# A diffusion block on one core: one of the seven block products of the MLP's second matrix product is itself made by seven inner products

## The chip, the cores and the metric

The kernel runs on one core of one Trainium2 chip. Its engines each work through a queue of their own: TensorE (PE in the profile, with its weight loads shown apart as PEld), VectorE (DVE), ScalarE (ACT), GpSimd (POOL) and SyncE (SP), which only issues transfers. The metric is the device time of one execution in microseconds. "Before" is the kernel without the change, 1021.87 us in the median of 3 runs (1021.27 to 1022.33).

## The reference, cut to what matters

One layer of a hybrid diffusion backbone. A token-mixing sub-layer (a pooling mixer and neighbourhood attention) comes first and is not touched; the second sub-layer is an MLP with a squared ReLU, on 1024 tokens of width 1024 with 4096 hidden columns, all in float32:

```python
def _sq_relu_mlp(h, w1, w2):
    return jnp.square(jax.nn.relu(h @ w1)) @ w2
...
    y_x = _sq_relu_mlp(_modulate(x, g_pre_mlp[l], sh2, sc2), w_mlp_in[l], w_mlp_out[l])
    x = x + gt2 * _rmsnorm(y_x, g_post_mlp[l])
```

The change concerns the second product alone: the hidden values (1024 x 4096) times `w_mlp_out` (4096 x 1024).

## The kernel before, in words

**Precision.** A float32 product is made of three matmuls in the fp32r type. Each operand is split into a high part (a cast, on ACT, `high_part`, L169) and a low part (operand minus high part, on DVE, `low_part`, L175), and `three` (L221 to L223) adds high x high, high x low and low x high in one PSUM bank.

**Seven block products.** The second product is cut in 2 x 2 blocks (512 tokens, 2048 hidden columns, 512 output columns) and made by Winograd's form of Strassen's method: the seven products P1 to P7 instead of eight. Their left operands are blocks of hidden values or sums of them (A11, A12, A22, S1 to S4), written to DRAM by the first product's stage (`keep`, on ACT's queue) and read back (`hidden`, tiles `hr...`, on SP's queue). Their right operands are blocks of `w_mlp_out` (`b11`, `b12`, `b21`, `b22`) or differences of them, made by DVE (L2047, L2049).

**Groups.** Each block product is 8 groups (g = 0 to 7) of 256 hidden columns. A group is 4 token tiles x 2 pieces x 3 matmuls, 24 matmuls of 128x512. P1 adds up in the four banks `pyx`, P6 in `pyy`; P2 is the block product A12 x b21, added in P1's banks, its groups between those of P6 (`items`). Then come P7, P5, P4 and P3 in the banks `pyv` and `pyz`.

**Order.** In this last stage PE, ACT, DVE and SP are held to the order in which the program is written (`in_order`); POOL's order is the scheduler's. Every group begins with `prepare()`, which writes down the loads, splits and sums for the group three items further on in the list `items`. So operands are made at most about three items ahead: the buffers of high and low weight parts (`whl`, 8 of 128x1024, four pairs) come free only when PE is through with the item four back. Raw weights have 4 buffers (`wraw`), raw hidden values 4 (`h`), and 33 pages (`act`) hold the rest. Loads are issued on SP's queue in the order of the program, so a load that waits for its buffer, or for an earlier transfer whose semaphore it is to use, holds up those behind it.

**The gate.** Among P1's groups the MLP's gate row is finished: before group 3 PE sums `accb` in the bank `pgb`, DVE multiplies it (L270), and POOL issues four small stores of it (`mod_out`, L276). Otherwise POOL has nothing to do in this stretch.

Of the kernel before, what the change touches and what calls it, by code (L numbers as in the profile page):

```python
# [11 lines left out]
F32 = mybir.dt.float32  # L12
# [91 lines left out]
def hybrid_block(ctx, tc, x, ctx_in, w_mod, mod_pages, w_u, b_mod, gp1, gp2, w_in, pool_w, rpb, w_out, w1, w2, vectors,  # L104
# [1414 lines left out]
    with tc.tile_pool(name="ps2", bufs=6, space=PSUM) as ps2:  # L1519

      def bank(name):
          if name[:3] == "phv" or name in ("poz_0", "poz_1") or name[:2] in ("px", "py") and name[-2:] in ("_3", "_7"):
              return lasting(name)
          return ps2.tile([P, 512], F32, tag="mm", name=name)

      with ExitStack() as tmp2:
# [257 lines left out]
        def second_steps(b12, b22):  # L1784
# [13 lines left out]
            for name in ("T2", "T1", "T3", "B22", "T4"):  # L1798
# [9 lines left out]
                for n in ("A11", "A12", "A22", "S1", "S2", "S3", "S4")}  # L1808
# [49 lines left out]
        def kept(name, p):  # L1858
            return hidd[name][p // 2][:, (p % 2) * 512 : (p % 2) * 512 + 512]
# [160 lines left out]
        def wcols(name, i, h, g):  # L2020
            return columns(wraw.tile([P, 1024], F32, tag="raw", name=f"{name}_{g}"), i, h, g)
# [15 lines left out]
        def operands(name, g, made=None):  # L2037
# [4 lines left out]
            if name == "P2":  # L2042
                return hidden("A12", g), made(f"b21_{g}", wcols("b21", 1, 0, g))
# [18 lines left out]

        AHEAD = 3
        items = [("P1", g) for g in range(NG)]
        for a, b in (("P6", "P2"), ("P7", "P5")):
            items += [(n, g) for g in range(NG) for n in (a, b)]
# [48 lines left out]
        with tc.issue_after(first[ET.PE]), in_order(ET.PE, ET.Activation, ET.DVE, ET.SP):  # L2115
# [67 lines left out]
            x = four("pyx")  # L2183
            for g in range(NG):
                if g == 1:
                    gain = mod_gain(gp2, page("gpb")[:, :256], nc.gpsimd)
                if g == 3:
                    mod_gate("b", acc_b[-1], gain, lambda name: pg)
                    mod_out("b", acc_b[-1])
                group(x, "P1", g)  # L2190
            s1 = halves("s1")
            for t in range(4):
                nc.scalar.copy(s1[t], x[t])
            y = four("pyy")
            for g in range(NG):
                group(y, "P6", g)
                if g == NG // 2:
                    G2 = gate_page("b")
                if g == NG - 1:
                    u2 = halves("u2")  # L2200
                    for t in range(4):
                        nc.vector.tensor_tensor(u2[t], y[t], s1[t], add)
                group(x, "P2", g, more=True)
            for t in range(4):
                rows[t] = page(f"row{t}")
                gated(t, 0, x[t])
# [93 lines left out]
```

## Time and profile before

| | us |
|---|---|
| median of 3 runs (lowest, highest) | 1021.87 (1021.27, 1022.33) |
| span of the profiled execution, first to last instruction | 1019.4 |
| what lies around the span (median less span) | 2.5 |
| PE busy in the span | 1008.7 |
| from P1's first matmul to P7's first | 131.3 |

The profiled execution's own time is known by its span alone, so a forecast is made against the span and 2.5 us are put on it. In the rows, buffer numbers are left out of names: `b_3l` is the low part of `b11` of group 3, `hhA_3h` the high part of its hidden block, and A11, A12 and A22 all read `hdA`, `hrA` or `hhA`. In a list of instructions the first number is the start and the second the duration, in us; a duration runs to the instruction's end, while the next one of a full queue starts a little earlier, so costs in a row of instructions are taken from start to start. `PEclk` is the granted share of TensorE's clock.

### The profile page before, as it was taken

What the parts mean: (1) busy time and instruction counts of PE and PEld (TensorE: products, weight loads), DVE (VectorE), ACT (ScalarE), POOL (GpSimd) and SP (SyncE); (2) the same over time, 40 slices, a digit from 0 to 9 for tenths busy, and PEclk for the clock granted to TensorE, in tenths of its full rate; (3) what the DMA queues carried; (4) which work ended last, traced back from release to release, by engine and by line L of the source; (5) the groups of instructions that cost most, each with busy time, mean ns of one, the idle gap of its engine ahead of it and who ended that gap; (6) DMA issues with size and microseconds to landing.
All of it is one profiled execution on the core that took longest, in us unless ns stands there. A gap on an engine that the chain in (4) does not pass through costs nothing.

```text
span 1019.4 us, 16277 instructions
## 1 busy us (share of the span) xinstructions
PE 1008.7 (99%) x6010; PEld 834.4 (82%) x6010; DVE 746.4 (73%) x1170; ACT 548.1 (54%) x964; POOL 154.5 (15%) x234
## 2 busy tenths in 40 slices
PE   8999999999999999999999999999999999999997
PEld 5788888878998888888888888888888888888886
DVE  5588767977885689879988888745757666557576
ACT  6672254348986746786555544555543343334442
POOL 4111210166774221410000000000000000000002
PEclk9999999999999999999999999999999999999999
DMA  9899798641448945885776657537967766556555
GB/s 368 314 295 305 256 265 293 206 104 43 96 95 204 232 183 187 297 216 197 256 260 208 213 194 225 177 135 251 347 218 261 248 228 214 200 167 203 169 184 226
DMA packets 117312, 222.72 MB, mean 218 GB/s; under 512 B 9521, under 2 KB 47281, under 8 KB 117233
## 3 DMA queue, kind: packets, MB, share of 16 engines
q1 hardware_dynamic: 90736, 171.14, 50.0%
q0 software_dynamic: 9360, 19.58, 9.3%
q10 hardware_dynamic: 17136, 30.97, 8.1%
q8 instruction: 47, 0.77, 0.3%
q14 instruction: 33, 0.26, 0.1%
HBM read 168.16 MB, written 52.45 MB: 216 GB/s over the span
## 4 chain that ended last, share of the span: by engine, by line
PE 96%; DMA 2%; DVE 1%; ACT 0%; issue 0%; SPq 0%; DVEq 0%; ACTq 0%
PE pu L476 4%; PE pa L1288 4%; PE S L1208 3%; PE phx L221 3%; PE phz L221 3%; PE phv L221 3%; PE pyx L221 3%; PE phx L223 3%; PE phx L222 3%; PE phv L223 3%; PE pyx L222 3%; PE pyz L221 3%; PE phz L223 3%; PE phv L222 3%; PE phz L222 3%; PE pyz L222 3%
## 5 line engine op out<-in xcount | busy, mean ns | idle before, releaser
L1234 ACT ACTIVATE sp<-sp,nm 128x640 f32<-128x640 f32 (+1 forms) x64 | 51.4, 802 | 10.9 <-DVE ri L1238 5.1
L1223 DVE CUSTOM_DVE_ANT_0 sp<-S,tab 128x640 f32<-128x640 f32 (+1 forms) x56 | 44.5, 795 | 13.9 <-PE pz L1254 9.5
L1855 ACT ACTIVATE c<-c 128x512 f32<-128x512 f32 x48 | 30.3, 632 | 44.8 <-DVE c L1975 25.6
L169 ACT CAST wpS<-S 128x512 fp32r<-128x512 f32 x64 | 38.7, 616 | 27.4 <-PE phv L223 9.7
L221 PE MATMUL phx<-thB,wpA 128*128 128x512 f32 x128 | 50.2, 392 | 0.0
L222 PE MATMUL phx<-tlB,wpA 128*128 128x512 f32 x128 | 49.8, 389 | 0.0
L223 PE MATMUL phx<-thB,wpA 128*128 128x512 f32 x128 | 49.8, 389 | 0.0
L175 DVE TENSOR_TENSOR wpS<-S,wpS 128x512 fp32r<-128x512 f32 x64 | 43.5, 688 | 7.6 <-ACT wpS L169 7.5
L163 POOL TENSOR_TENSOR ry<-vy,nhalf 128x1 f32<-128x1 f32 x7 | 5.4, 767 | 275.6 <-DVE vy L161 275.6
L1856 ACT ACTIVATE c<-c 128x512 f32<-128x512 f32 x48 | 30.3, 631 | 15.1 <-DVE sa L1938 12.1
L221 PEld LDWEIGHTS phx<-thB,wpA 128*128 128x128 f32 x128 | 24.0, 188 | 5.5 <-ACT s L1906 0.4
L223 PEld LDWEIGHTS phx<-thB,wpA 128*128 128x128 f32 x128 | 24.0, 188 | 5.0
L222 PEld LDWEIGHTS phx<-tlB,wpA 128*128 128x128 f32 x128 | 24.0, 188 | 4.9
L1273 DVE COPY pt<-T 128x512 f32<-128x512 f32 x32 | 22.0, 687 | 5.5 <-PE T L1254 5.5
L1288 PE MATMUL pa<-pt,v 128*64 128x128 f32 x352 | 25.9, 279 | 0.2
L221 PE MATMUL phv<-thT,wpA 128*128 128x512 f32 x64 | 25.0, 391 | 0.0
L221 PE MATMUL phz<-thB,wpS 128*128 128x512 f32 x64 | 25.0, 391 | 0.0
L223 PE MATMUL phv<-thT,wpA 128*128 128x512 f32 x64 | 24.9, 389 | 0.0
L222 PE MATMUL phz<-tlB,wpS 128*128 128x512 f32 x64 | 24.9, 389 | 0.0
L222 PE MATMUL phv<-tlT,wpA 128*128 128x512 f32 x64 | 24.9, 389 | 0.0
L221 PE MATMUL phy<-thT,wpS 128*128 128x512 f32 x64 | 24.9, 389 | 0.0
L222 PE MATMUL phy<-tlT,wpS 128*128 128x512 f32 x64 | 24.9, 389 | 0.0
(1179 smaller groups left out, 3442.6 us busy)
## 6 DMA issues: line engine op xcount, KB each, us to landing
b<-in_w SPq DMA_DIRECT2D x64, 512.0 KB, 4.3
hrS<-hdS SPq DMA_DIRECT2D x32, 512.0 KB, 5.1
hrA<-hdA SPq DMA_DIRECT2D x24, 512.0 KB, 5.6
wm<-in_mod_pages SPq DMA_DIRECT2D x16, 512.0 KB, 9.3
wa_0w<-in_w SPq DMA_DIRECT2D x16, 512.0 KB, 5.0
wa_1w<-in_w SPq DMA_DIRECT2D x16, 512.0 KB, 4.3
hdA<-c ACTq DMA_DIRECT2D x32, 256.0 KB, 2.2
hdS<-sa ACTq DMA_DIRECT2D x32, 256.0 KB, 2.2
```

The costliest lines, as they stand in the source:

```text
L169: nc.scalar.copy(hi, src)
L175: nc.vector.tensor_tensor(lo, src, hi.bitcast(F32), sub)
L221: nc.tensor.matmul(ps, ahi, bhi, start=first, stop=False, skip_group_check=more)
L222: nc.tensor.matmul(ps, ahi, blo, start=False, stop=False, skip_group_check=more)
L223: nc.tensor.matmul(ps, alo, bhi, start=False, stop=last, skip_group_check=more)
L476: nc.tensor.matmul(pus[b][j], wk(wgt, k, low, j * P, P), r, start=(k == 0 and n == 0), stop=(k == KT - 1 and n == 2))
L1208: nc.tensor.matmul(S[e][:, c0 : c0 + k[0].shape[1]], q[n_q][hs, cols], k[n_k][hs], start=(n_q + n_k == 0), stop=(n_q == 1))
L1223: nc.vector.tensor_tensor_reduce(out=to, in0=s, in1=bt, scale=1.0, scalar=BIG, op0=add, op1=ALU.min, accum_out=nm)
L1234: nc.scalar.activation(sp, sp, AF.Exp, bias=least[i, e], scale=-1.0, accum_out=sums[i][:, e : e + 1])
L1288: nc.tensor.matmul(pa[e * HD : (e + 1) * HD, cols], v[:, f : f + HD], turns[i][:, e, c] if c < 4 else fifths[i][:, :, (e + 1) * HD : (e + ...
L1855: nc.scalar.activation(r, src, AF.Relu)
L1856: nc.scalar.activation(r, r, AF.Square)
```

## The change

P2 is itself cut in 2 x 2 (256 tokens, 1024 hidden columns, 256 output columns) and made by seven inner products M1 to M7, in the same form. Each is made in two halves (h = 0, 1) of 512 hidden columns: 2 token tiles x 4 pieces x 3 matmuls, 24 matmuls of 128x256, all of one inner product in a single bank `pyi...`. The 14 halves stand no longer between P6's groups but among P1's and P6's: after P1's group 2 the order is M1 M1, P1, M5, P1, M5 M6, P1, M6, P1, M4 M4, P1 (the last group), M2 M2, P6, M3, P6, M3 M7, P6, M7, P6, and then P6's groups 4 to 7.

Left and right operands of an inner product are quarters of A12 and b21, or sums of such. Every half loads quarters of 512 KB (14 loads per h, 28 in all, where P2 had 16), the sums are made by POOL on 128x1024 (`inner_operands`: two for M5, two for M6, one for M4, one for M3, two for M7, for each h), and each half is split as before, on ACT and DVE. A12 is stored in two tensors `hidq` of DRAM instead of eight. Results are taken from the banks by ACT and DVE into pages (`inner_kept`), one sum of 128x512 among them by POOL, and the four row blocks that P1 and P2 together gave are added up by POOL (128x512, four) and not in PSUM. P1's and P6's last bank no longer stand in the two lasting banks, which the inner products use.

**POOL's queue around the gate's four loads (L266).** `accb` is the gate's sum and `gb` its stores; `Si`, `Ti` and `S1i` are pages that are kept, and the number behind them is h. Before:

```order
L238 MEMSET accb_7168 128x1024
L239 DMA accb_7168<-in_b_mod 1x16x64
L266 DMA gpb_8128<-in_gp2 32x256 x4
L276 DMA gb_8210<-accb_7168 16x1x16 x4
L163 TENSOR_TENSOR ry_0_10109<-vy_0_10107,nhalf_79 128x1
```

With the change:

```order
L266 DMA gpb_8122<-in_gp2 32x256 x4
L2086 TENSOR_TENSOR S1i_0_8199<-S1i_0_8199,a11M5_0_8201 128x1024
L2068 TENSOR_TENSOR Si_0_8086<-S1i_0_8199,Si_0_8086 128x1024
L2068 TENSOR_TENSOR Ti_0_8088<-b01M5_0_8203,Ti_0_8088 128x1024
L276 DMA gb_8283<-accb_7162 16x1x16 x4
L2086 TENSOR_TENSOR S1i_1_8288<-S1i_1_8288,a11M5_1_8290 128x1024
L2068 TENSOR_TENSOR Si_1_8127<-S1i_1_8288,Si_1_8127 128x1024
L2068 TENSOR_TENSOR Ti_1_8129<-b01M5_1_8292,Ti_1_8129 128x1024
L2068 TENSOR_TENSOR Ti_0_8088<-b11M6_0_8328,Ti_0_8088 128x1024
```

M6's left operand (`Si`) is made between M5's left (`S1i`) and right (`Ti`), and the gate's stores stand between the two halves of M5.

**DVE's queue at the same place.** `hhM5_0l` and `wM5_0l` are the low parts of M5's left and right operand for h = 0. With the change:

```order
L175 TENSOR_TENSOR hhM5_0l_8208<-S1i_0_8199,hhM5_0h_8207 128x1024
L175 TENSOR_TENSOR wM5_0l_8212<-Ti_0_8088,wM5_0h_8211 128x1024
L175 TENSOR_TENSOR hhA11_4l_8245<-hrA11_4_8242,hhA11_4h_8244 128x1024
L175 TENSOR_TENSOR b11_4l_8249<-b11_4_8240,b11_4h_8248 128x1024
L270 TENSOR_TENSOR accb_7162<-pgb_8081,gpb_8122 128x256
L175 TENSOR_TENSOR hhM5_1l_8297<-S1i_1_8288,hhM5_1h_8296 128x1024
L175 TENSOR_TENSOR wM5_1l_8301<-Ti_1_8129,wM5_1h_8300 128x1024
L175 TENSOR_TENSOR hhM6_0l_8333<-Si_0_8086,hhM6_0h_8332 128x1024
```

The gate's product, which POOL's stores wait for, is now behind both low parts of M5's first half and of P1's group 4.

## The diff

```diff
@@ -1519,7 +1519,8 @@
     with tc.tile_pool(name="ps2", bufs=6, space=PSUM) as ps2:
 
       def bank(name):
-          if name[:3] == "phv" or name in ("poz_0", "poz_1") or name[:2] in ("px", "py") and name[-2:] in ("_3", "_7"):
+          if (name[:3] in ("phv", "pyi") or name in ("poz_0", "poz_1") or name[:2] == "px" and name[-2:] in ("_3", "_7")
+                  or name in ("pyv_3", "pyz_3")):
               return lasting(name)
           return ps2.tile([P, 512], F32, tag="mm", name=name)
 
@@ -1805,7 +1806,8 @@
         EARLY, SPILLED = 10, 6
 
         hidd = {n: [dram.tile([P, 1024], F32, tag=f"hd{n}_{g}", name=f"hd{n}_{g}") for g in range(NPAIR // 2)]
-                for n in ("A11", "A12", "A22", "S1", "S2", "S3", "S4")}
+                for n in ("A11", "A22", "S1", "S2", "S3", "S4")}
+        hidq = [dram.tile([P, 4, 1024], F32, tag=f"hq{h}", name=f"hq{h}") for h in range(2)]
 
         s1d = [dram.tile([P, 512], F32, tag=f"s1_{p}", name=f"s1_{p}") for p in range(SPILLED)]
 
@@ -1856,6 +1858,8 @@
             nc.scalar.activation(r, r, AF.Square)
 
         def kept(name, p):
+            if name == "A12":
+                return hidq[p // 8][:, p // 2 % 4, (p % 2) * 512 : (p % 2) * 512 + 512]
             return hidd[name][p // 2][:, (p % 2) * 512 : (p % 2) * 512 + 512]
 
 
@@ -2039,8 +2043,8 @@
             if name == "P1":
                 t1[g] = columns(page(f"b11_{g}"), 0, 0, g)
                 return hidden("A11", g, g <= AHEAD + 1), made(f"b11_{g}", t1[g])
-            if name == "P2":
-                return hidden("A12", g), made(f"b21_{g}", wcols("b21", 1, 0, g))
+            if name in INNER:
+                return inner_operands(name, g)
             if name == "P6":
 
                 b12, b22 = wcols("b12", 0, 1, g), wcols("b22", 1, 1, g)
@@ -2060,10 +2064,53 @@
             nc.vector.tensor_tensor(b21, b21, t2[g], sub)
             return hidden("A22", g), made(f"t4_{g}", b21)
 
+        INNER = ("M1", "M5", "M6", "M4", "M2", "M3", "M7")
+        kept_raw, subtract = {}, lambda to, a, b: nc.gpsimd.tensor_tensor(to, a, b, sub)
+
+        def inner_raw(name, left, r, c, h, at=None):
+            if at is None:
+                at = tmp.tile([P, 1024], F32, tag="h", name=name, bufs=4) if left else wraw.tile([P, 1024], F32, tag="raw", name=name)
+            nc.sync.dma_start(at.rearrange("p (a f) -> p a f", a=4),
+                              hidq[h][:, :, c * 512 + r * 256 : c * 512 + r * 256 + 256] if left else
+                              w2v[1][:, 8 * h + r : 8 * h + 8 : 2, c * 256 : (c + 1) * 256])
+            return at
+
+        def inner_operands(name, h):
+            a = lambda r, c, at=None: inner_raw(f"a{r}{c}{name}_{h}", True, r, c, h, at)
+            b = lambda r, c, at=None: inner_raw(f"b{r}{c}{name}_{h}", False, r, c, h, at)
+            new = lambda n: kept_raw.setdefault((n, h), page(f"{n}i_{h}"))
+            if name == "M1":
+                x, y = a(0, 0, new("S")), b(0, 0, new("T"))
+            elif name == "M5":
+                x, more, y, less = a(1, 0, new("S1")), a(1, 1), kept_raw["T", h], b(0, 1)
+                nc.gpsimd.tensor_tensor(x, x, more, add)
+                subtract(y, less, y)
+            elif name == "M6":
+                x, y, z = kept_raw["S", h], kept_raw["T", h], b(1, 1)
+                subtract(x, kept_raw.pop(("S1", h)), x)
+                subtract(y, z, y)
+            elif name == "M4":
+                x, z, y = a(1, 1), b(1, 0, new("B21")), kept_raw.pop(("T", h))
+                subtract(y, z, y)
+            elif name == "M2":
+                x, y = a(0, 1, new("A12")), kept_raw.pop(("B21", h))
+            elif name == "M3":
+                x, z, y = kept_raw.pop(("S", h)), kept_raw.pop(("A12", h)), b(1, 1)
+                subtract(x, z, x)
+            else:
+                x, z, y, less = a(0, 0), a(1, 0), b(1, 1), b(0, 1)
+                subtract(x, x, z)
+                subtract(y, y, less)
+            return split_pages(f"hh{name}_{h}", x), high_low(f"w{name}_{h}", y)
+
         AHEAD = 3
-        items = [("P1", g) for g in range(NG)]
-        for a, b in (("P6", "P2"), ("P7", "P5")):
-            items += [(n, g) for g in range(NG) for n in (a, b)]
+        inner = iter([(n, h) for n in INNER for h in range(2)])
+        items = [("P1", g) for g in range(3)]
+        for n, i in zip((2, 1, 2, 1, 2, 2, 1, 2, 1), [("P1", g) for g in range(3, NG)] + [("P6", g) for g in range(4)]):
+            items += [*islice(inner, n), i]
+        items += [("P6", g) for g in range(4, NG)]
+        assert next(inner, None) is None
+        items += [(n, g) for g in range(NG) for n in ("P7", "P5")]
         items += [(n, g) for g in range(NG // 2) for n in ("P4", "P3")] + [("P3", g) for g in range(NG // 2, NG)]
         items += [("P4", g) for g in range(NG // 2, NG)]
         made = {}
@@ -2180,30 +2227,78 @@
 
 
             pg = bank("pgb")
-            x = four("pyx")
-            for g in range(NG):
-                if g == 1:
-                    gain = mod_gain(gp2, page("gpb")[:, :256], nc.gpsimd)
-                if g == 3:
-                    mod_gate("b", acc_b[-1], gain, lambda name: pg)
-                    mod_out("b", acc_b[-1])
-                group(x, "P1", g)
-            s1 = halves("s1")
+            inner_banks, parts = {}, {}
+            by_two = lambda v: v.rearrange("p (t n) -> p t n", t=2)
+
+            def inner_part(name):
+                if name not in parts:
+                    parts[name] = page(f"{name}i")
+                return parts[name]
+
+            block = lambda r, c: by_two(inner_part(f"c{r}"))[:, :, c * 256 : (c + 1) * 256]
+            held = lambda n: inner_part("tu"[n // 2])[:, n % 2 * 512 : n % 2 * 512 + 512]
+
+            def inner_kept(name, ps):
+                plus = lambda to, a, b: nc.vector.tensor_tensor(to, a, b, add)
+                if name == "M1":
+                    nc.scalar.copy(held(0), ps)
+                elif name == "M5":
+                    nc.scalar.copy(held(1), ps)
+                elif name == "M6":
+                    plus(held(2), ps, held(0))
+                    nc.gpsimd.tensor_tensor(held(3), held(2), held(1), add)
+                elif name == "M4":
+                    plus(block(1, 0), by_two(ps), by_two(held(2)))
+                elif name == "M2":
+                    plus(block(0, 0), by_two(ps), by_two(held(0)))
+                elif name == "M3":
+                    plus(block(0, 1), by_two(ps), by_two(held(3)))
+                else:
+                    plus(block(1, 0), by_two(ps), block(1, 0))
+                    plus(block(1, 1), by_two(ps), by_two(held(3)))
+
+            def inner_group(name, h):
+                prepare()
+                a, w = made.pop((name, h))
+                if h == 0:
+                    inner_banks[name] = bank(f"pyi{name}")
+                ps = inner_banks[name]
+                for t in range(2):
+                    for j in range(4):
+                        ts, cs = slice(j * 256 + t * P, j * 256 + (t + 1) * P), slice(j * 256, (j + 1) * 256)
+                        three(ps[:, t * 256 : (t + 1) * 256], a[0][:, ts], a[1][:, ts], w[0][:, cs], w[1][:, cs],
+                              h + t + j == 0, h == 1 and j == 3, more=t > 0)
+                if h == 1:
+                    inner_kept(name, ps)
+
+            x, y = four("pyx"), None
+            for name, g in items[: items.index(("P7", 0))]:
+                if name in INNER:
+                    inner_group(name, g)
+                elif name == "P1":
+                    if g == 1:
+                        gain = mod_gain(gp2, page("gpb")[:, :256], nc.gpsimd)
+                    if g == 3:
+                        mod_gate("b", acc_b[-1], gain, lambda name: pg)
+                        mod_out("b", acc_b[-1])
+                    group(x, "P1", g)
+                    if g == NG - 1:
+                        s1 = halves("s1")
+                        for t in range(4):
+                            nc.scalar.copy(s1[t], x[t])
+                        y = four("pyy")
+                else:
+                    group(y, "P6", g)
+                    if g == NG // 2:
+                        G2 = gate_page("b")
+            u2 = halves("u2")
             for t in range(4):
-                nc.scalar.copy(s1[t], x[t])
-            y = four("pyy")
-            for g in range(NG):
-                group(y, "P6", g)
-                if g == NG // 2:
-                    G2 = gate_page("b")
-                if g == NG - 1:
-                    u2 = halves("u2")
-                    for t in range(4):
-                        nc.vector.tensor_tensor(u2[t], y[t], s1[t], add)
-                group(x, "P2", g, more=True)
+                nc.vector.tensor_tensor(u2[t], y[t], s1[t], add)
             for t in range(4):
+                c = inner_part(f"c{t // 2}")[:, t % 2 * 512 : t % 2 * 512 + 512]
+                nc.gpsimd.tensor_tensor(c, c, s1[t], add)
                 rows[t] = page(f"row{t}")
-                gated(t, 0, x[t])
+                gated(t, 0, c)
             v, z = four("pyv"), four("pyz")
             for g in range(NG):
                 group(v, "P7", g)
```

## The prediction

> **What bounds the kernel now.** I read the page's busy shares first, then the stage's windows, then its instructions.
>
> ```profile
> span 1019.4 us, 16277 instructions
> PE 1008.7 (99%) x6010; PEld 834.4 (82%) x6010; DVE 746.4 (73%) x1170; ACT 548.1 (54%) x964; POOL 154.5 (15%) x234
> 707.80:752.10 44.30, 44.30 (x201) 36.11 (x200) 31.11 (x30) 22.43 (x25) 1.93 (x4) 1.00 0.83 295
> 752.10:839.10 87.00, 87.00 (x385) 72.06 (x384) 57.87 (x52) 34.38 (x39) 0.00 (x0) 1.00 0.71 240
> L221 PE MATMUL pyx<-b_0h,hhA_0h x16: 389/389/389, 707.8 to 762.3; 128*128 128x512 f32 x16
> L221 PE MATMUL pyv<-t_0h,hhS_0h x8: 389/389/389, 839.1 to 843.9; 128*128 128x512 f32 x8
> ```
>
> The two windows are P1's eight groups and then P6's and P2's sixteen (length, then busy time of PE, PEld, DVE, ACT, POOL, the granted clock, DMA's busy share, GB/s). PE is busy in all of both, so this stretch lasts as long as its matmuls; DVE is free for a third of it, POOL nearly all of it. The two tile rows give the stretch's ends: 839.1 - 707.8 = 131.3 us.
>
> **The matmuls.** The tail of the kernel already has this shape, 128x256 with a new weight load for each:
>
> ```profile
> 762.99 0.39 PE L221 MATMUL pyy<-t_1h,hhS_1h 128*128 128x512 f32 x1
> 768.43 0.39 PE L221 MATMUL pyx<-b_1h,hhA_1h 128*128 128x512 f32 x1
> 1010.66 0.28 PE L221 MATMUL pyw<-t_4h,hhA_4h 128*128 128x256 f32 x1
> 1013.42 0.28 PE L223 MATMUL pyw<-t_7h,hhA_7l 128*128 128x256 f32 x1
> ```
>
> The first two rows are 24 matmuls apart: 5.44 us a group, 0.2267 us for 512 columns. The last two are the first and last of 24: 2.76 / 23 = 0.1200 us for 256. P2 goes, 8 x 5.44 = 43.5 us; 14 halves of 24 x 0.12 = 2.88 us come, 40.3 us. **The gain on PE is 3.2 us**, all there is to gain. P1's eight groups took 44.3 us, 0.8 more than 8 x 5.44; that is the gate's sum.
>
> **What the halves need.** Splits and POOL's sums are costed by these rows:
>
> ```profile
> 716.45 1.22 DVE L175 TENSOR_TENSOR hhA_3l<-hrA,hhA_3h 128x1024 fp32r<-128x1024 f32 x1
> 717.58 1.22 DVE L175 TENSOR_TENSOR b_3l<-b,b_3h 128x1024 fp32r<-128x1024 f32 x1
> 756.15 1.22 DVE L2047 TENSOR_TENSOR b<-b,b 128x1024 f32<-128x1024 f32 x1
> 758.55 1.22 DVE L175 TENSOR_TENSOR hhS_2l<-hrS,hhS_2h 128x1024 fp32r<-128x1024 f32 x1
> 715.00 1.04 ACT L169 CAST hhA_3h<-hrA 128x1024 fp32r<-128x1024 f32 x1
> 715.95 1.05 ACT L169 CAST b_3h<-b 128x1024 fp32r<-128x1024 f32 x1
> 222.98 1.28 POOL L1091 TENSOR_TENSOR qP<-q,qP 128x512 fp32r<-128x512 f32 x1
> 224.22 0.28 POOL L1240 COPY rb<-ri 128x128 f32<-128x128 f32 x1
> 261.20 2.50 POOL L1077 TENSOR_TENSOR tab<-msk,U 128x128 f32<-128x128 f32 x6
> L276 POOL DMA_DIRECT2D gb<-accb x4 | 1.9, 490 | 27.3 <-DVE accb L270 27.3
> 725.99 0.42 DVE L270 TENSOR_TENSOR accb<-pgb,gpb 128x256 f32<-128x256 f32 x1
> ```
>
> From start to start: a low part 1.14 us, P6's two differences with the gap 2.40, a cast 0.95, the gate's four stores 1.96 of POOL's queue. POOL has no 128x1024 sum in this trace. Its 128x512 takes 1.25, its 128x128 2.50 / 6 = 0.42; the line through both gives 2.37 us. Twice the 512 row is 2.5; the slope without the fixed part, 2.23. I take 2.37.
>
> **The term that decides: DVE and POOL exclude each other.** Where both worked on operands in SBUF, the timeline reads:
>
> ```profile
> 211.89 0.68 DVE L175 TENSOR_TENSOR qP<-q,qP 128x512 fp32r<-128x512 f32 x1
> 212.01 1.71 POOL L1091 TENSOR_TENSOR qP<-q,qP 128x512 fp32r<-128x512 f32 x1
> 212.49 1.78 DVE L175 TENSOR_TENSOR kP0l<-kT,kP0h 128x512 fp32r<-128x512 f32 x1
> 214.19 0.67 DVE L1138 TENSOR_TENSOR q<-q,pqv 128x512 f32<-128x512 f32 x1
> 220.47 1.29 POOL L1091 TENSOR_TENSOR kP2l<-kT,kP2h 128x512 fp32r<-128x512 f32 x1 [2.67 <-ACT kP2h L1090]
> 220.61 0.69 DVE L1140 TENSOR_TENSOR q<-pqv,q 128x512 f32<-128x512 f32 x1 [0.47 <-PE pqv L223]
> 15.30 0.69 DVE L463 TENSOR_TENSOR hx<-xT,hx 128x512 fp32r<-128x512 f32 x1
> 15.56 1.58 POOL L502 TENSOR_TENSOR wu0l<-wu0w,wu0h 128x512 fp32r<-128x512 f32 x1 [2.04 <-ACT wu0h L169]
> ```
>
> POOL begins at 212.01 beside a low part of DVE and takes 1.71 instead of 1.28: 0.43 longer, about what DVE still had to do. DVE's next low part, due at 212.49, takes 1.78 instead of 0.68 and so starts in truth at about 213.6, when POOL is done. At 220.61 the same two engines don't disturb each other: there DVE reads one operand from PSUM (`pqv`). At 15.56 POOL again waits for DVE. So a DVE sum of two SBUF operands and a POOL sum run one after the other, in turn. In the stretch changed, every low part and P6's differences are such sums, and so are all of POOL's. What looks free in the windows isn't free for both at once.
>
> *First place, M5.* Its loads stand in SP's queue where these stood:
>
> ```profile
> 711.18 0.38 ACTq L1876 DMA_DIRECT2D hdA<-c  x1
> 712.72 0.33 ACTq L1876 DMA_DIRECT2D hdS<-sb  x1
> 719.10 0.34 SPq L2033 DMA_DIRECT2D hrA<-hdA  x1
> 720.05 0.38 SPq L2033 DMA_DIRECT2D hrA<-hdA  x1
> b<-in_w SPq DMA_DIRECT2D x40, 512.0 KB, 5.1
> SPq L2033 <- DMA hdA<-c: 11.9, 2, 7.5
> ```
>
> They wait for the landing of the last two stores, until 719.1 and 720.05, and land some 5 us later, at 725.1. Then S1 2.37, S 2.37, DVE's low part between 1.14, T 2.37, cast 0.95, low part 1.14: 735.4. PE comes to M5 at 707.8 + 3 x 5.44 + 2 x 2.88 + 0.8 + 5.44 = 736.1. Just in time. But DVE now makes P1's group 4 (2 x 1.14) and the gate's product (0.35), and only then may POOL issue the four stores (1.96), make S1 and S of h = 1 (4.74), let DVE's low part pass (1.14), make T (2.37) and, before DVE gets its turn, M6's T (2.37), and the last low part ends (1.22): 16.4 us, at 751.8. PE is at M5's second half at 736.1 + 2.88 + 5.44 = 744.4 and **stands for some 7 us**.
>
> *The whole stretch.* After that the two engines' sums set the pace. From 735.4 until the operands of P6's group 6 are made there are 22 items with two low parts each, 44 x 1.14 = 50.2; seven pairs of differences, 16.8; 13 sums of POOL on 128x1024, 30.8; five on 128x512, 6.3. That is 104 us, one after the other. To it come the gate's stores, 2.0, while DVE has nothing it could do, and six sums from PSUM in DVE's order, about 4. So 735.4 + 110 = 845.4. Without a wait PE would start P6's group 6 at 839.1 - 3.2 - 2 x 5.44 = 825.0. It starts 20.4 us later, and P7 at 845.4 + 10.9 = 856.3 instead of 839.1: **17 us later than before**, the gain on PE included.
>
> Behind P7 nothing changes on PE, and POOL's four last sums and the rows they feed aren't needed before the end. ACT's casts (28 where P2 had 16, 0.95 each) lie beside DVE's low parts; 12 loads of 512 KB are added, 6.3 MB in a stretch that moved 240 to 295 GB/s, hidden as long as DVE and POOL are later than they. Bounds: with POOL at 2.23 and no idle time beyond the 104 us, 102 us, +9; with POOL at 2.5 and 6 us more of waiting for casts, +25. I take +17, since stores, PSUM sums and turns are all in DVE's and POOL's orders. Sum: 1019.4 + 17 + 2.5 around the span = **1039 us**; the forecast's own range is 1031 to 1047.
>
> **Rivals.** *No exclusion (same).* If the rows at 212 are something else, M5's chain alone remains: ready at 734.3, then 2.28 + 0.35 + 1.96 + 3 x 2.37 + 0.95 + 1.22 = 13.9, at 748.2: a wait of 3.8 against the gain of 3.2, 1022.5 us. Against it: all three overlaps quoted fit. *A clean gain (faster).* If besides POOL needs under 2 us, M5 is in time as well: 1019.4 - 3.2 + 2.5 = 1018.7. Against it, POOL's rows. *The clock falls (slower still).* PE never stood for 5 us in this trace (`PEclk` 1.00 in both windows); with waits of 7 us it may. A group of 24 matmuls at half speed costs 2.9 us more; two such places, partly hidden behind DVE and POOL, 1039 + 4 = 1043. The Trainium skill's page "TensorE: Matmul & The Clock Gate", Part 1, says that about 3.4 us of idle time halve the clock and that it takes as long to come back; no row of this trace shows it, and by it alone the sum would be 1.7 us more for each long wait. *Loads become the bound (slower).* From M3 to P6's group 3 there are 19 loads, 10 MB, in 27.8 us of PE's time: 358 GB/s, above both windows. If they land 3 us late at three items, 1022 + 9 - 3 = 1028. But a PE that waits for DVE and POOL gives them time. That the change doesn't do what it says I exclude: the shapes are in the order.
>
> **How the numbers follow.** Exclusion as worked out 0.68; with a fallen clock 0.14; loads alone 0.05; no exclusion 0.09; clean gain 0.04. Faster or slower means by over 0.2%, 2.0 us, about what runs of this kernel can tell from no change. Slower 0.87, same 0.09, faster 0.04. The range takes in the clock's case and the lower bound with the loads' case: 1027 to 1047.
>
> **What would show it.** In the changed profile: 128x256 matmuls 0.120 us apart; PE waiting for DVE low parts of M5's second half (6 to 7 us), and again at P6's groups 1 to 3; DVE's low parts of 1.22 us becoming 2 to 3.6 us where a POOL sum lies beside them, and POOL's sums 2.4 to 3.5; P7's first matmul some 149 us after P1's. Low parts that stay at 1.22 us beside POOL's sums would make the prediction wrong, and so would DVE idle while PE waits.

## The result, and the profile after

The changed kernel takes 1045.68 us in the median of 5 runs (1042.59 to 1047.35), the kernel before 1021.69 us beside it (1021.27 to 1022.33). The ratio is 1.0231, with a 95% interval of 1.0217 to 1.0245: 24 us slower. The profiled execution took 1043.92 us. The head of its page, and its two windows on either side of P7's first matmul (length, then busy time of PE, PEld, DVE, ACT, POOL, the granted clock, DMA's busy share, GB/s):

```profile
span 1042.1 us, 16697 instructions
PE 1015.6 (97%) x6154; PEld 844.4 (81%) x6154; DVE 786.1 (75%) x1188; ACT 560.9 (54%) x978; POOL 211.7 (20%) x255
...
708.10:860.00 151.90, 137.72 (x729) 118.31 (x728) 122.72 (x92) 66.59 (x71) 58.69 (x25) 0.94 0.74 252
860.00:1042.10 182.10, 174.90 (x793) 145.26 (x792) 121.33 (x132) 73.78 (x100) 5.37 (x7) 0.99 0.58 204
```

The stretch from P1's first matmul to P7's first, 131.3 us before, is now 151.9 us, and PE is no longer busy in all of it. What follows P7's first matmul took 180.3 us before and takes 182.1. So 20.6 of the lost microseconds lie ahead of P7. The six largest waits of PE from 700 us on (total, times, longest):

```profile
PE pyiM L221 <- ACT wM_1h L169: 6.0, 2, 5.2
PE pyiM L222 <- DVE wM_1l L175: 3.4, 3, 1.7
PE pyy L222 <- DVE t_3l L175: 1.7, 1, 1.7
PE pyv L221 <- DVE u L2296: 1.0, 1, 1.0
PE pyy L222 <- DVE t_2l L175: 1.0, 1, 1.0
PE pyx L222 <- DVE b_5l L175: 0.9, 1, 0.9
```

The longest, 5.2 + 1.7 us, is the second half of M5 (`wM_1`, operand of h = 1). The rest is at P1's group 5 (`b_5l`), M3 and M7 (`wM_1` again), P6's groups 2 and 3 (`t_2l`, `t_3l`) and, behind P7's first matmul, at `u`.

POOL around M5 and DVE beside it, in the same profile (start, duration; in brackets the idle time before and what ended it):

```profile
738.84 1.95 POOL L276 DMA_DIRECT2D gb<-accb  x4 [5.24 <-DVE accb L270]
740.81 2.41 POOL L2086 TENSOR_TENSOR S1i<-S1i,a11M 128x1024 f32<-128x1024 f32 x1
...
745.63 3.33 POOL L2068 TENSOR_TENSOR Ti<-b01M,Ti 128x1024 f32<-128x1024 f32 x1
```

```profile
734.72 1.23 DVE L175 TENSOR_TENSOR wM_0l<-Ti,wM_0h 128x1024 fp32r<-128x1024 f32 x1 [3.38 <-ACT wM_0h L169]
...
744.34 2.43 DVE L175 TENSOR_TENSOR hhM_1l<-S1i,hhM_1h 128x1024 fp32r<-128x1024 f32 x1 [5.79 <-ACT hhM_1h L169]
750.07 2.28 DVE L175 TENSOR_TENSOR wM_1l<-Ti,wM_1h 128x1024 fp32r<-128x1024 f32 x1 [3.31 <-ACT wM_1h L169]
...
753.41 3.40 DVE L175 TENSOR_TENSOR wM_0l<-Ti,wM_0h 128x1024 fp32r<-128x1024 f32 x1
...
818.16 1.23 DVE L175 TENSOR_TENSOR hhM_1l<-a00M,hhM_1h 128x1024 fp32r<-128x1024 f32 x1 [3.36 <-ACT hhM_1h L169]
822.75 1.23 DVE L175 TENSOR_TENSOR wM_1l<-b11M,wM_1h 128x1024 fp32r<-128x1024 f32 x1 [3.36 <-ACT wM_1h L169]
```

Two things are to be seen. A POOL sum takes 2.41 us by itself and 3.33 us where it starts beside a low part of DVE; a low part takes 1.22 us by itself and 2.3 to 3.4 us beside a POOL sum. And DVE stands idle, 5.79 and 3.31 us at M5, twice 3.36 us at M7, because the operand that is next in its order isn't there: POOL's sums come one after the other, behind the gate's stores at M5, behind late loads at M7. Which of the two, the exclusion or POOL's chain, costs the time was the question for the experiments.

### The profile page after: what moved, and what is told of

Read it like the earlier page. It is cut to its first block, busy times and chain, and to the rows that moved or that the text cites. A ratio compares the mean times of both kernels' runs of the same rounds, so it can differ in the third digit from the quotient of the medians.

```text
span 1042.1 us, 16697 instructions
## 1 busy us (share of the span) xinstructions
PE 1015.6 (97%) x6154; PEld 844.4 (81%) x6154; DVE 786.1 (75%) x1188; ACT 560.9 (54%) x978; POOL 211.7 (20%) x255
## 5 line engine op out<-in xcount | busy, mean ns | idle before, releaser
L221 PE MATMUL phv<-thT,wpA 128*128 128x512 f32 x64 | 25.0, 391 | 0.0
```

The lines of the kernel that those rows point to most:

```text
L221: nc.tensor.matmul(ps, ahi, bhi, start=first, stop=False, skip_group_check=more)
```

## The experiments

The kernel before was timed again beside runs 1 to 12, with medians of 1020.85 to 1021.21 us, and each ratio is against the one beside it. The intervals reach 1 to 2 us to either side, so differences of a microsecond between two medians say little. "P1 to P7" is the time from P1's first matmul to P7's first in the profiled execution.

| kernel | median us | ratio (95%) | P1 to P7, us |
|---|---|---|---|
| before | 1021.69 | 1 | 131.3 |
| changed | 1045.68 | 1.0231 (1.0217 to 1.0245) | 151.9 |
| 1: all sums on DVE | 1022.60 | 1.0013 (1.0003 to 1.0022) | 133.0 |
| 2: gate one group earlier | 1039.70 | 1.0187 (1.0170 to 1.0204) | 148.0 |
| 3: filler matmuls in the waits | 1043.10 | 1.0214 (1.0199 to 1.0229) | 152.2 |
| 4: before, with POOL sums | 1022.07 | 1.0011 (1.0002 to 1.0020) | 132.0 |
| 5: before, with POOL copies | 1021.57 | (one run) | 131.3 |
| 6: POOL copies for sums | 1022.06 | 1.0009 (1.0000 to 1.0018) | 130.2 |
| 7: memsets for sums | 1033.14 | 1.0111 (1.0096 to 1.0127) | 143.3 |
| 8: the same, shorter | 1031.81 | 1.0101 (1.0082 to 1.0121) | 141.7 |
| 9: 8 with the gate earlier | 1021.88 | 1.0009 (0.9999 to 1.0019) | 133.2 |
| 10: 1 with M3 and M7 later | 1020.71 | 0.9998 (0.9988 to 1.0008) | 128.9 |
| 11: 1 with M5 to M2 earlier | 1019.88 | 0.9986 (0.9977 to 0.9996) | 130.0 |
| 12: 11 with M7's end and u moved | 1018.27 | 0.9971 (0.9960 to 0.9981) | 128.3 |

**1. All sums on DVE.** (POOL has 21 sums in the changed kernel, 16 of 128x1024 and 5 of 128x512; some of the expectations miscount them.)

```diff
-kept_raw, subtract = {}, lambda to, a, b: nc.gpsimd.tensor_tensor(to, a, b, sub)
+kept_raw, subtract = {}, lambda to, a, b: nc.vector.tensor_tensor(to, a, b, sub)
...   (likewise the sum of S1, held(3) and the four c)
```

> The changed kernel with all of its 23 sums of POOL given to DVE, nothing else altered. Exclusion (the forecast's reason: DVE's two-operand sums in SBUF and POOL's sums go one at a time): a sum costs DVE 1.2 us instead of 2.4 us of both engines, the low parts return to 1.22 us, the waits of PE at the second half of M5 and at P6 groups 1 to 3 go, and so the clock stays up: P7's first matmul 128 to 136 us after P1's instead of 151.9, the time 1018 to 1026. Rival, the queues (the gate's four stores on POOL's queue and the chain of S, T hold up the operands, whoever sums): the wait at M5 stays, 1036 to 1042. Rival, the loads (operands come too late for anybody): PE's waits move to the sums on DVE and its loads, 1028 or more. Rival, DVE is full: 27 us of sums are added to an engine that must do the low parts, 1030 to 1045.

Measured: 1022.60 us, P1 to P7 133.0 us. The 23 us are gone, though DVE now has 110 instructions in the stretch instead of 92. Its window from P1 to P7 and all of PE's waits from 690 us on:

```profile
707.60:840.60 133.00, 130.68 (x730) 113.74 (x729) 120.68 (x110) 68.07 (x72) 1.94 (x4) 0.99 0.85 292
```

```profile
PE pyy L221 <- ACT t_3h L169: 1.1, 1, 1.1
PE pyy L222 <- DVE t_3l L175: 0.8, 1, 0.8
PE pyiM L222 <- DVE wM_1l L175: 0.5, 1, 0.5
```

M5's wait is gone too, with the gate's stores and the loads where they were, so neither of these makes it without POOL's sums, and DVE isn't full. The same loads keep up at 292 GB/s, where the changed kernel had 252: they are no bound here. But this edit takes away two things at once, the exclusion and a chain of sums of 2.4 us each, and doesn't tell them apart.

**2. The gate earlier.**

```diff
-                    if g == 3:
+                    if g == 2:
                         mod_gate("b", acc_b[-1], gain, lambda name: pg)
```

> The changed kernel with the gate's product and its four stores one group earlier (ahead of P1's group 2 instead of group 3), so that they are out of POOL's queue before the sums of M5. If the chain through the gate sets the first place: the wait of 5.6 + 2.3 us at the second half of M5 shrinks to below 3 us, its 1.9 us of half-speed matmuls go, and P7 starts 4 to 8 us earlier unless the later places take it back. If the whole stretch's tally of exclusive work decides (104 us by the forecast), the waits only move to P6's groups 1 to 3: time 1042 to 1046, as the changed kernel. With the chain alone at work: 1036 to 1041.

Measured: 1039.70 us, P1 to P7 148.0, in the chain's range. Its waits:

```profile
PE pyx L222 <- DVE b_4l L175: 3.4, 1, 3.4
PE pyiM L221 <- ACT wM_1h L169: 2.7, 1, 2.7
PE pyy L222 <- DVE t_3l L175: 1.7, 1, 1.7
```

The wait at the second half of M5 is gone (the 2.7 us are M7's), but 3.4 us of it come back one item earlier: POOL's sums for M5's second half now run while DVE makes the low parts of P1's group 4, and `hhA_4l`, `b_4l` and `hhM_1l` take 3.42, 3.36 and 3.40 us in a row. So the place is made by the chain, and the exclusion eats part of what a shorter chain would give.

**3. Filler matmuls.** Where PE would wait it multiplies operands that are at hand, into the gate's bank that nobody reads any more.

```diff
+                for _ in range({("M5", 0): 33, ("M7", 0): 10, ("M7", 1): 15}.get((name, h), 0)):
+                    nc.tensor.matmul(pg, a[0][:, :P], w[0][:, :512], start=True, stop=True)
```

> The changed kernel with matmuls that nobody reads, of 128x512, where TensorE would else wait: 33 (7.5 us) behind the first half of M5, 10 (2.3 us) behind the first half of M7, 15 (3.4 us) behind its second half. TensorE has no idle time there, so the clock should not fall. If the fallen clock (0.213 us for 128x256, 0.427 us for 128x512 after the waits) costs the time that the forecast missed: 2 to 5 us faster than the changed kernel, 1041 to 1044, and the spacing stays 0.120 and 0.227 us. If the slow matmuls only fill time in which the next operands are late anyway: within 1 us of the changed kernel. If the filler delays real work: 1046 to 1050.

Measured: 1043.10 us, 2.6 less than the changed kernel in the median and within the range expected if the slow matmuls cost time. But the intervals of the two ratios overlap, and P1 to P7 in the profiled execution is 152.2 against 151.9 us:

```profile
707.00:859.20 152.20, 145.09 (x787) 124.87 (x786) 124.34 (x92) 66.69 (x71) 58.27 (x25) 0.99 0.75 250
```

The granted clock in the stretch is 0.99 instead of 0.94; only 15 matmuls of M7 were still slow. The stretch is as long as in the changed kernel. So in this pair of profiles the slow matmuls filled time in which the next operands weren't made yet. The medians leave more room: the changed kernel's executions go from 1042.59 us at a mean granted clock of 0.992 to 1047.35 us at 0.989, and the profiled one, 1043.92 us at 0.991, lies below their median. Whether the fallen clock costs some of the 2.6 us stays open.

**4 and 5. POOL's work alone, in the kernel before.** For each group of P1, P6 and P2 one POOL operation on the weights just loaded, into a page that nobody reads: a sum in the first, a copy in the second.

```diff
+                beside(b12, b22)          # nc.gpsimd.tensor_tensor(spare[0], a, b, add)
+                                          # or nc.gpsimd.tensor_copy(spare[0], a)
                 nc.vector.tensor_tensor(t1[g], b12, t1[g], sub)
```

> The kernel before with one sum of 128x1024 on POOL for each group of P1, P6 and P2 (24 of them), from two SBUF operands that a low part or a sum of DVE reads too, into a spare page that nobody reads. Exclusion: the low parts and sums of DVE beside a POOL sum take 2 to 3.6 us instead of 1.2 us, POOL's sums up to 3.4 us instead of 2.4 us; 24 sums of 2.4 us are 58 us of exclusive time in the 131 us of these products, on top of some 60 us of DVE's, so that TensorE waits little or not: 1022 to 1030. No exclusion (the lows of the changed kernel are slow for their own operands' sake): the lows stay at 1.22 us and the time at 1022.

> The kernel before with one copy of 128x1024 on POOL (one operand in SBUF) for each group of P1, P6 and P2, where the run before this had sums of two operands. If only two operands exclude DVE's sums: low parts beside the copies 1.22 us, copies all of one duration, 1 to 2.4 us. If any work of POOL on SBUF does: low parts of 2 us and more, as beside the sums.

Measured: 1022.07 and 1021.57 us. The window from P1 to P7, then rows of DVE and of POOL, all of the kernel with the sums:

```profile
707.50:839.50 132.00, 131.68 (x585) 108.14 (x584) 126.10 (x82) 57.45 (x65) 56.57 (x24) 1.00 0.74 259
```

```profile
735.92 3.41 DVE L2058 TENSOR_TENSOR b<-b,b 128x1024 f32<-128x1024 f32 x1
...
743.34 3.32 DVE L175 TENSOR_TENSOR t_0l<-t,t_0h 128x1024 fp32r<-128x1024 f32 x1
```

```profile
734.99 3.26 POOL L2042 TENSOR_TENSOR spare<-b,b 128x1024 f32<-128x1024 f32 x1
```

The exclusion is there without any inner product, as forecast. DVE's busy time between P1 and P7 goes from 89.0 to 126.1 us, and yet the kernel is only about 1 us slower: PE waits 0.3 us in all. DVE is three items ahead, and no operand waits for POOL. So the exclusion by itself isn't a loss. That it becomes one where the items that need both engines come faster than these can serve them is what the two kernels together suggest; no run varied the lead alone. The copies run 1.04 us where no low part lies beside them, 1.44 us in the mean of 23, and DVE's busy time over the whole span is 761 us instead of 746.

**6. Copies for sums.** In the changed kernel each sum of POOL becomes a copy of one operand; the sum is left out.

```diff
-lambda to, a, b: nc.gpsimd.tensor_tensor(to, a, b, sub)
+lambda to, a, b: nc.gpsimd.tensor_copy(to, b if to is a else a)
```

> The changed kernel with each of POOL's 19 sums (14 of 128x1024, 5 of 128x512) made a copy of one of its two operands, in the same place, behind the same loads and of the same size. The sum itself is left out, so the second block of the product is not computed. POOL's chain (S1, S, T and the gate's stores in one queue, the loads of M7 behind them) is all still there; only POOL's second operand in SBUF is gone. If the exclusion is one of two-operand sums, the low parts beside a copy stay at 1.22 us; what then remains of the 20.6 us between P1 and P7 is the price of the chain: with copies of about 2 us, a wait at the second half of M5 of 1 to 4 us, 1022 to 1032. If the exclusion takes in copies too, lows of 2 to 3.5 us and 1036 to 1044. If the chain of POOL alone costs what was lost, and the exclusion is a by-product, the waits at M5 and M7 stay as they are if copies take some 2.4 us: 1038 to 1044.

Measured: 1022.06 us. It was meant to keep POOL's chain and lift the exclusion, and it did neither, so none of the three cases came true as a whole (the low parts are those of the second, the time is that of the first):

```profile
738.97 1.04 POOL L2068 COPY Ti<-b01M 128x1024 f32<-128x1024 f32 x1
739.96 2.04 POOL L2068 COPY Ti<-b11M 128x1024 f32<-128x1024 f32 x1
```

```profile
743.00 1.21 DVE L175 TENSOR_TENSOR hhM_0l<-Si,hhM_0h 128x1024 fp32r<-128x1024 f32 x1
744.13 2.05 DVE L175 TENSOR_TENSOR wM_0l<-Ti,wM_0h 128x1024 fp32r<-128x1024 f32 x1
```

A copy takes 1.04 us, not 2.4, and it still shuts DVE's sums out (2.05 us), though it has one operand. What it shows is that the change costs almost nothing when POOL's part is short, exclusion or not. It doesn't separate the two causes.

**7, 8 and 9. POOL's time without the exclusion.** Each sum becomes a one-column copy that ties it to the same loads, and memsets of the result, in the same order on POOL's queue. The sums are left out. In 7 there are two and a half memsets of 128x1024, in 8 two and an eighth, because in 7 a stand-in took 2.8 us with its tie where a sum takes 2.4. Run 9 is run 8 with the gate one group earlier.

```diff
+        def for_sum(to, *read, n=1024):
+            for i, r in enumerate(read):
+                nc.gpsimd.tensor_copy(to[:, i : i + 1], r[:, :1])
+            for part in (to, to, to[:, : n // 2]):      # in 8 and 9: n // 8
+                nc.gpsimd.memset(part, 0.0)
```

> The changed kernel with each of POOL's sums made two and a half memsets of its result (0.95 us for 128x1024 in the kernel before, beside a low part of DVE that keeps its 1.22 us) behind one-column copies that tie it to the same loads, in the same order on POOL's queue. The sums themselves are left out, so the second block of the product is not computed. POOL then works as long for each sum as it does alone (2.4 us) and its chain S1, S, T with the gate's stores stays, but it doesn't shut DVE out. If the exclusion is what costs: low parts 1.22 us throughout; a wait of about 4 us at the second half of M5, as the rival without exclusion had it, and some at M7; P7's first matmul 131 to 138 us after P1's, 1022 to 1028. If the length of POOL's chain costs and DVE's longer low parts are a by-product: waits and time as in the changed kernel, 1036 to 1044, P7 some 145 to 150 us after P1.

> The run with memsets in place of POOL's sums, made 0.4 us shorter each: there a sum's stand-in took 2.8 to 3.0 us of POOL with its tie, where the sum by itself takes 2.40. The second block of the product is not computed here either. With exclusion gone and POOL's chain at its real length: the wait at the second half of M5 shrinks from 7.3 us by 3 times 0.4 and what the first half starts earlier, to 4 to 6 us, and the time from 1033.1 to 1028 to 1031 us: then the exclusion is worth about two thirds of the 24 us and POOL's chain one third. If the wait doesn't shrink with the chain's length, something else makes the operands late there, and the time stays at 1033.

> The same, with the gate's product and stores ahead of P1's group 2, out of the chain of M5 (the sums are left out as before). If without exclusion all that is left is M5's chain: the wait at its second half falls by 3 to 6 us against the run beside it, P7's first matmul 130 to 135 us after P1's, 1021 to 1026. If what is left lies elsewhere (M7's loads, P6's groups), at most 2 us.

Measured: 1033.14, 1031.81 and 1021.88 us. Run 7 lies between its two ranges and run 8 is 0.8 us above the first of its two; run 9 is inside its range. In all three the low parts take 1.22 us throughout, beside memsets as well. Run 8's POOL and DVE at M5, and the two largest waits of its PE:

```profile
740.84 1.96 POOL L2071 MEMSET S1i<- 128x1024 f32 x2
...
749.43 2.22 POOL L2071 MEMSET Ti<- 128x1024 f32 x3
```

```profile
750.24 1.23 DVE L175 TENSOR_TENSOR wM_1l<-Ti,wM_1h 128x1024 fp32r<-128x1024 f32 x1 [4.83 <-ACT wM_1h L169]
```

```profile
PE pyiM L221 <- ACT wM_1h L169: 6.1, 2, 6.0
PE pyiM L222 <- DVE wM_1l L175: 1.6, 2, 0.9
```

M5's wait is nearly as long without the exclusion (6.0 + 0.7 us; the 0.9 is M7's) as with it (5.2 + 1.7), and the operand comes at nearly the same time: low part from 750.24 us here; in the changed kernel from 750.07 us by its row, in truth from 751.3, when M6's sum on POOL ends (748.92 + 2.35). So POOL's chain alone, as the stand-ins make it, gives such a wait. Run 9 takes the gate out of the chain and the wait is gone; its two largest are those of M5's first half:

```profile
PE pyiM L222 <- DVE wM_0l L175: 0.9, 1, 0.9
PE pyiM L221 <- ACT wM_0h L169: 0.9, 1, 0.9
```

So the 24 us split: 13.9 us go with the exclusion (1045.68 to 1031.81), 9.9 us with M5's chain through the gate's stores (1031.81 to 1021.88), each to about 2 us. The stand-ins aren't exact. In run 8 one tie, inside the sum of S, took 1.2 us beside a low part, so the chain's share is put rather too high. And the shares depend on the order in which they are taken: with the exclusion in place the earlier gate is worth 6.0 us (run 2), and the exclusion then 17.8 (1039.70 to 1021.88).

**10, 11 and 12. A version that gains.** From run 1 on, with all sums on DVE, only the places of the halves were changed. The numbers say how many halves stand ahead of P1's groups 3 to 7 and P6's groups 0 and on.

```diff
-zip((2, 1, 2, 1, 2, 2, 1, 2, 1), ...)
+zip((2, 1, 2, 1, 2, 2, 1, 1, 1, 1), ...)      # run 10
+zip((2, 2, 2, 2, 2, 1, 1, 1, 0, 1), ...)      # run 11
+zip((2, 2, 2, 2, 2, 1, 1, 1, 0, 0, 0, 0, 0), ...)   # run 12; M7's second half behind P6's group 7,
+                                                    # and u's four sums ahead of it
```

> The kernel with all sums on DVE (1022.6 us, where TensorE waits 1.3 + 1.0 us at P6's group 3 and then runs nine matmuls at half speed, 5.2 us in all above 0.120 and 0.227 us a matmul), with the second half of M3 and both of M7 each one group later, so that no two halves lie between groups of P6. If DVE's work per group is what is late there, the wait goes, and the 3.2 us gained on TensorE show: 1017 to 1020. If the loads are late there (16 engines were busy for 95% of that stretch), the wait moves with M7: 1021 to 1023.

> The same kernel with two halves behind each of P1's groups 3 to 7 (M1 to M2 done there), M3 and M7 single ones among P6's groups 0 to 4. DVE has 3 us free in each group of P1 and 0.6 us in each of P6. If DVE's free time decides: 1017 to 1020, as or better than the late one. If the loads decide (they were busy for all of the time between P1's groups 4 and 7): new waits of 2 to 5 us within P1, 1022 to 1027.

> All sums on DVE, two halves behind each of P1's groups 3 to 7, M3 and M7's first half singly among P6's first groups, M7's second half behind P6's last group, and the sums of u, which P7's third token tile waits for (1.1 to 1.4 us of TensorE in every changed kernel), ahead of it. If that wait is from the sums' place alone, it goes, and with it the one at P6's group 4: P7's first matmul 128 to 129 us after P1's, 1018 to 1019.5, 0.998 of the kernel before. If P7's first operands are late instead (DVE has u, M7's blocks and P7's first low parts together), the wait only moves: 1020 to 1022.

Measured: 1020.71, 1019.88 and 1018.27 us. Run 10's wait at P6's group 3 is gone and its profiled stretch is 128.9 us, but its median lies between the two ranges expected, and its ratio is no different from 1. Runs 11 and 12 are inside theirs. In run 11 the halves crowded into P1 cost no wait there (its waits are at P6's group 4 and at `u`), so DVE's free time decided and not the loads. In run 12 PE has no wait at all in the stretch:

```profile
707.60:835.90 128.30, 128.30 (x730) 112.57 (x729) 116.51 (x106) 65.89 (x70) 1.93 (x4) 1.00 0.87 295
835.90:1016.50 180.60, 174.62 (x793) 145.23 (x792) 126.03 (x139) 75.18 (x101) 5.38 (x7) 0.99 0.60 209
```

It beats the kernel before by 0.29% (0.19 to 0.40%). P1 to P7 is 3.0 us shorter than before, and what follows P7's first matmul is back to 180.6 us.

## Why the prediction was right, and where it was off

**Right, by its own steps.** *The matmuls.* The gain of 3.2 us is real and all there is: run 12, without waits, shows 131.3 - 128.3 = 3.0 us. *POOL's sum.* 2.37 us were taken, 2.35 to 2.42 measured where no sum of DVE lay beside it; the gate's stores 1.96 taken, 1.95 measured. *The exclusion.* It is there as the rows at 212 us had it, in the changed kernel and in run 4, and runs 7 to 9, where POOL's memsets read nothing, have low parts of 1.22 us. The Trainium skill, page "SBUF — State Buffer", section "Who interferes with whom", says the same: a DVE instruction with two inputs in SBUF contends with a GpSimd instruction that reads SBUF, not with one that only writes it. Runs 4, 6 and 8 agree on each of the three: 3.41 us beside a sum, 2.05 us beside a copy, 1.23 us beside a memset. *M5.* The first half's operands were forecast for 735.4 us and PE for 736.1; the last low part ends at 734.72 + 1.23 = 735.95 and PE begins at 736.4. The second half was forecast for 751.8 us; its last low part ends at 750.07 + 2.28 = 752.35. PE waits 5.2 + 1.7 us where "some 7 us" were said. But the exclusion was named as the term that decides, and by the runs it is 13.9 or 17.8 of the 24 us, by the order. And 1045.7 us lies 1.3 us from the upper end of the range: that it is inside is partly luck.

**Off in size: the whole stretch.** The step gave 110 us from the first half of M5 to the low parts of P6's group 6: 104 of exclusive work and 6 in which neither engine works on it. The profile has `t_6l` ending at 848.8 us, 113.4 us after 735.4. The exclusive work in it, counted from the instructions of both engines, covers 102.6 us (all time in which POOL made a sum or DVE one of two SBUF operands), 1.4 less than said; the time without any is 10.8 us, 4.8 more. What was said is there, 2.6 us at the gate's stores and the sums from PSUM; new are four stands of 0.9 to 1.7 us, 4.8 in all, at M3, P6's group 2 and M7, where DVE's next low part waits for its cast while POOL makes no sum. So P7 starts 151.9 us after P1 instead of 148.5. Nor does the tally alone set the pace: by it an earlier gate could save the 2.0 us of its stores, while run 2's stretch is 3.9 us shorter. The prediction named DVE idle while PE waits as a sign against it; at M5 and M7 that is what is seen, though the sums of POOL that DVE waits for there are part of the tally.

**Wrong: nothing changes behind P7.** It takes 1.8 us longer. The sums `u` of P6's banks used to be made beside P2's last group. Now P6's last group is followed at once by P7, whose third token tile needs a bank that `u` must first empty, and DVE comes to `u` only 3.0 us after P6's last matmul (863.2 against 860.2 us): PE waits 1.0 of the 1.8 us for it. In run 12 the sums are moved, the wait is gone, and the stretch takes 180.6 us. The place isn't all of it: in run 1, with `u` where the change put it, DVE comes to it 1.1 us after P6's last matmul, PE doesn't wait, and the stretch takes 180.5 us. That `u`'s place was moved is in the change; the prediction didn't follow it.

**The rest of the miss.** Around the span 2.5 us were taken and 1.8 measured (1043.92 - 1042.1), P1 begins 0.3 us later, and the median lies 1.8 us above the profiled execution. With the 3.4 and 1.8 us this gives 3.4 + 1.8 + 0.3 - 0.7 + 1.8 = 6.6 us of the 6.7 from 1039 to 1045.7.

**The rivals.** *No exclusion* was priced at 1022.5 us, and that price was wrong by 9 us: without the exclusion the kernel takes 1031.8 us (run 8). The step that failed is the wait of 3.8 us at M5. It reckoned the first half ready at 734.3 us, and from there 13.9 us to 748.2. In run 8 the first half is ready at 735.8 us and the second at 751.5: the later start is 1.5 us, the rest mainly POOL's sum of S, 3.5 us with its tie instead of 2.4. On top come matmuls at half speed behind the wait (18 of them, 0.213 instead of 0.120 us: 1.7 us), waits at M7 and P6's group 3, and 1.5 us behind P7. So the term that was said to decide isn't alone: exclusion about 14 us, chain about 10. *The clock falls.* It does fall, as that rival said: the stretch has 0.94. Its price of 4 us on top isn't seen in the profiles of run 3; whether some of the 2.6 us between the medians is its stays open. *Loads.* Run 1 moves the same loads in less time without a wait for them. In the changed kernel POOL's sums of M7 did wait for loads, but these were issued late: SP stood for 32.7 us in all (six times, at most 20.3) until P6's differences on DVE had freed a buffer, and the loads of M7's first half stood behind the longest of these waits. So by SP's waits the delay came from DVE there too; it wasn't tried by itself.

## What to carry to other kernels

Before giving idle POOL elementwise work, count POOL's reads and DVE's two-operand sums in SBUF as one engine, and count them stage by stage: run 4 hid 24 sums behind a lead of three items, while the changed kernel lost 24 us on 21 sums whose results PE was waiting for. A sum of 128x1024 costs DVE 1.22 us and POOL 2.40 us plus what DVE then loses, so here a DVE that was busy for 68% of the stretch before (89.0 of 131.3 us), and for 91% with all the sums (120.7 of 133.0 us in run 1), was still the better place. When work is put among the groups of a product, place it by what its operands cost per group, and look at what used to lie under the group that it replaced (here `u`).

## What the runs showed of the hardware that was not expected

**The clock fell after waits far shorter than forecast.** TensorE behind M5's wait in the changed kernel (start, duration):

```profile
750.09 0.58 PE L221 MATMUL pyiM<-wM_1h,hhM_1h 128*128 128x256 f32 x1 [5.16 <-ACT wM_1h L169]
752.41 0.58 PE L222 MATMUL pyiM<-wM_1l,hhM_1h 128*128 128x256 f32 x1 [1.74 <-DVE wM_1l L175]
...
753.00 0.41 PE L221 MATMUL pyiM<-wM_1h,hhM_1h 128*128 128x256 f32 x1
753.22 0.41 PE L222 MATMUL pyiM<-wM_1l,hhM_1h 128*128 128x256 f32 x1
...
757.00 0.28 PE L222 MATMUL pyiM<-wM_1l,hhM_1h 128*128 128x256 f32 x1
757.12 0.28 PE L223 MATMUL pyiM<-wM_1h,hhM_1l 128*128 128x256 f32 x1
```

They are 0.213 us apart until 756.85 us and 0.12 us from 757.0 on. The same happened in run 1 after waits of only 1.10 and 0.76 us, one behind the other:

```profile
810.63 0.49 PE L221 MATMUL pyy<-t_3h,hhS_3h 128*128 128x512 f32 x1 [1.10 <-ACT t_3h L169]
811.89 0.63 PE L222 MATMUL pyy<-t_3l,hhS_3h 128*128 128x512 f32 x1 [0.76 <-DVE t_3l L175]
812.32 0.63 PE L223 MATMUL pyy<-t_3h,hhS_3l 128*128 128x512 f32 x1
```

and not in run 8, at the same instructions after waits of the same length:

```profile
820.65 0.49 PE L221 MATMUL pyy<-t_3h,hhS_3h 128*128 128x512 f32 x1 [1.12 <-ACT t_3h L169]
821.91 0.50 PE L222 MATMUL pyy<-t_3l,hhS_3h 128*128 128x512 f32 x1 [0.77 <-DVE t_3l L175]
822.25 0.39 PE L223 MATMUL pyy<-t_3h,hhS_3l 128*128 128x512 f32 x1
```

So two waits of about 1 us each can halve the clock for some 3 us, and needn't. What decides it is how they lie in time. The traces record the granted clock, and up to the tail each of its stretches, at full or at half, lasts a whole multiple of 3.413 us (at half 3.41, 6.83 and, in run 7, 10.24 us). So every run can be cut into windows of 3.413 us in step with its clock. Here are the two windows of run 1 around its waits, then two of run 8 (length, busy time of PE, PEld, DVE, ACT, POOL, the granted clock, DMA's busy share, GB/s):

```profile
808.69:812.10 3.41, 1.54 (x9) 1.03 (x9) 3.38 (x4) 1.71 (x2) 0.00 (x0) 1.00 1.02 368
812.10:815.51 3.41, 3.41 (x9) 2.64 (x9) 3.33 (x4) 1.43 (x2) 0.00 (x0) 0.50 1.00 350
```

```profile
817.26:820.67 3.41, 2.29 (x21) 2.09 (x19) 3.35 (x4) 1.04 (x1) 2.01 (x6) 1.00 0.88 306
820.67:824.08 3.41, 2.65 (x10) 1.96 (x11) 3.38 (x3) 1.05 (x1) 0.00 (x0) 1.00 1.03 369
```

In run 1 both waits fall into one window, in which PE stands for 1.87 us, and the next window has the half clock throughout. In run 8 an edge lies between them (1.12 and 0.76 us), and the clock stays. In all traces of this case, up to 1010 us, a window at full clock in which PE stood for 1.87 us or more (there are nine) was always followed by one at half clock, and one with 1.36 us or less never was; in between, windows with 1.55, 1.69 and 1.73 us were, and another with 1.73 us wasn't. The ends of matmuls are modelled in the profile, so the limit is no sharper than that. The Trainium skill, page "TensorE: Matmul & The Clock Gate", Part 1, speaks of an idle window of about 3.4 us that runs freely, without regard to the kernel. The traces agree with the window's length and its running freely, but it needn't be idle throughout: 1.87 of 3.41 us were enough.

**Copies on POOL exclude DVE's sums as sums do, memsets don't** (2.05, 3.4 and 1.22 us for a low part beside them). And a POOL copy of 128x1024 takes 1.04 us, a sum 2.40, so what POOL needs for a second operand is more than the first operand costs.
